# Linear attention with a block-diagonal state: both heads' sequential and low-rank products padded with zeros to the whole 128x128 array

## The chip, the cores and the metric

The kernel runs on one core of a Trainium2 chip. The metric is the device time of one execution in microseconds. TensorE is PE in the rows (PEld its weight loads), VectorE is DVE, ScalarE is ACT, GpSimd is POOL, SyncE is SP and issues the DMAs.

## The reference

256 tokens of width 1024 go through two layers of a block A and then two of a block B. The part that the change touches is one of three branches of the mixing stage of block A, a linear attention with a state (RWKV-7): 8 heads of 64 features, and per head a 64x64 state that is carried over the tokens.

```python
def wkv7_scan(r, decay, k, v, a, b):
...
    def step(state, inp):
        r_t, w_t, k_t, v_t, a_t, b_t = inp
        sa = jnp.einsum('bhij,bhj->bhi', state, a_t)
        state = (state * w_t[:, :, None, :] + sa[..., None] * b_t[:, :, None, :]
                 + v_t[..., None] * k_t[:, :, None, :])
        return state, jnp.einsum('bhij,bhj->bhi', state, r_t)
...
    w = -jax.nn.softplus(-(w0 + jnp.tanh(xw) @ w_up)) - 0.5
    a = jax.nn.sigmoid(a0 + xa @ a_up)
```

The last two lines are the low-rank products: `xw` and `xa` have 64 features each.

## The kernel before

Features lie on partitions, tokens along the free dimension. Every large product is split into three matmuls of reduced-precision halves (lines 164, 165 and 166, `float32r`, 128x128 weights by 256 tokens); this stream of large products runs through the whole kernel. `wload` brings weights by DMA into a ring of buffers, ACT rounds them to `hi` (line 137) and DVE takes the rest `lo` (line 138).

The mixing stage `mix_a` puts small chains of dependent steps between the large products. Each chain is a generator, and `Order` decides in program order where its next step is emitted; the tile scheduler then fixes each engine's order. Four chains `rwkv_pair` per layer do the linear attention, each for two heads on the two halves of the 128 partitions; their products are in `float32`, which the trace records as two passes each. A chain forms the low-rank products (lines 460 and 473, 64 rows by 256 columns), the stacked keys `BK` and queries `AR`, the products inside the four chunks of 64 tokens (line 539), a triangular inverse `Q` by doubling (lines 582 and 590, products of 64x64), and then walks the chunks in order. In the walk each chunk reads the state `ST` (line 609, one product per head, each followed by its own addition into `W`, line 611), multiplies by the inverse (line 616, copied to `U` by line 618), updates the state (line 624; lines 628 to 631 on DVE) and forms the output (lines 636 and 638, in turn for each head, copied to `y` by line 640).

A head occupies 64 partitions, so these products use a quarter or a half of the array; `tile_size` of an instruction (64x64, 128x64, 64x128 or 128x128, rows by columns) says which form the array then has. The form stands in the rows as 64\*64 and so on. PSUM banks of the chains are `rec`, two in turn. The state is kept as [(head, feature), 64], the two heads under each other.

## Time and profile before

| what | value |
| --- | --- |
| median of 3 runs | 2324.88 us (2322.84 to 2325.23) |
| span of the profiled execution, first to last instruction | 2323.2 us |
| PE busy | 2240.6 us, 96% of the span |
| DVE busy | 1677.5 us, 72% |
| ACT busy | 1276.9 us, 55% |
| the chain that ended last | 80% PE, 8% DMA, 7% DVE, 4% ACT |

The profiled execution's span is its own time without what lies around the first and last instruction; the median of the runs is 1.7 us above it. Matmuls overlap in the pipeline, so durations of PE rows overlap too: what a product costs the stream is read from the starts of the rows, not from their durations. A start in the timeline is in microseconds from the span's start, and a row with xN merges N records.

### The profile page before, as it was taken

The numbers are of one execution on the slowest core, as the hardware profiler recorded it, in microseconds if no ns is written. First come the engines' busy times: TensorE is split into PE (matmuls) and PEld (weight loads), VectorE is DVE, ScalarE is ACT, GpSimd is POOL, SyncE is SP. The second block draws the span as 40 slices with busy tenths as digits, with TensorE's granted clock in tenths as the row PEclk, the third lists the DMA queues.
The fourth block names the chain that finished last, engine by engine and source line by source line (L and its number), as shares of the span: only waits on it lengthen the run. The fifth ranks groups of instructions, "written<-read, shape, count | busy, mean of one in ns | idle before, by whom it ended". The sixth has DMA issues, their size and how long they took to land.

```text
span 2323.2 us, 46766 instructions
## 1 busy us (share of the span) xinstructions
PE 2240.6 (96%) x19122; PEld 2142.4 (92%) x19122; DVE 1677.5 (72%) x3026; ACT 1276.9 (55%) x2144; POOL 0.2 (0%) x4
## 2 busy tenths in 40 slices
PE   4999998978999999999999999999999999999999
PEld 4888898978888889999999999899999999999999
DVE  7777767757677776877576659976667655997665
ACT  4574545544457464565454457654455446666444
POOL 0000000000000000000000000000000000000000
PEclk9999999989999999999999999999999999999999
DMA  7634457777663445875576563466565556346653
GB/s 294 190 118 128 142 177 242 250 199 231 191 199 116 137 129 167 266 228 159 169 237 182 161 208 109 131 211 186 156 210 183 174 168 200 109 138 216 183 158 124
DMA packets 129117, 416.69 MB, mean 179 GB/s; under 512 B 14564, under 2 KB 20324, under 8 KB 128134
## 3 DMA queue, kind: packets, MB, share of 16 engines
q1 hardware_dynamic: 126718, 409.50, 55.8%
q10 hardware_dynamic: 2184, 4.19, 0.9%
q8 instruction: 150, 2.46, 0.4%
q14 instruction: 65, 0.53, 0.1%
HBM read 408.40 MB, written 5.24 MB: 178 GB/s over the span
## 4 chain that ended last, share of the span: by engine, by line
PE 80%; DMA 8%; DVE 7%; ACT 4%; issue 1%; SPq 0%; ACTq 0%; DVEq 0%
PE ps L164 23%; PE ps L165 22%; PE ps L166 22%; DMA raw<-in_ffn_up 3%; DVE lo L138 2%; DMA raw<-in_w_ada 2%; ACT hi L137 1%; DMA raw<-in_w_in 1%; PE rec L582 1%; PE rec L590 1%; DVE raw L369 1%; PE rec L1178 1%; DVE raw L338 1%; PE rec L636 1%; PE ps L191 1%
## 5 line engine op out<-in xcount | busy, mean ns | idle before, releaser
L164 PE MATMUL ps<-h,hi 128*128 128x256 f32 x5080 | 1438.4, 284 | 31.9 <-ACT h L201 29.6
L166 PE MATMUL ps<-h,lo 128*128 128x256 f32 x5080 | 1433.4, 283 | 14.7 <-DVE lo L138 14.7
L165 PE MATMUL ps<-l,hi 128*128 128x256 f32 x5080 | 1435.7, 283 | 4.9 <-DVE l L202 4.7
L137 ACT CAST hi<-raw 128x1024 fp32r<-128x1024 f32 (+1 forms) x724 | 704.7, 977 | 648.4 <-PE ps L165 377.8
L138 DVE TENSOR_TENSOR lo<-raw,hi 128x1024 fp32r<-128x1024 f32 (+1 forms) x724 | 818.9, 1133 | 301.6 <-ACT hi L137 299.0
L164 PEld LDWEIGHTS ps<-h,hi 128*128 128x128 f32 x5080 | 961.0, 190 | 47.2 <-ACT h L201 31.9
L166 PEld LDWEIGHTS ps<-h,lo 128*128 128x128 f32 x5080 | 962.3, 190 | 23.8 <-DVE lo L138 15.7
L165 PEld LDWEIGHTS ps<-l,hi 128*128 128x128 f32 x5080 | 961.8, 189 | 13.9 <-DVE l L202 6.8
L201 ACT CAST h<-t 128x256 fp32r<-128x256 f32 x172 | 68.6, 403 | 122.8 <-DVE t L996 96.1
L338 DVE SCALAR_TENSOR_TENSOR raw<-raw,cact 128x1024 f32<-128x1024 f32 x80 | 97.2, 1215 | 35.4 <-DMA raw<-in_w_ada 35.4
L202 DVE TENSOR_TENSOR l<-t,h 128x256 fp32r<-128x256 f32 x172 | 72.3, 423 | 60.5 <-ACT h L201 59.9
L993 DVE TENSOR_TENSOR t<-ps,r 128x512 f32<-128x512 f32 x88 | 60.8, 690 | 41.7 <-PE ps L166 41.3
L1183 DVE SCALAR_TENSOR_TENSOR cy<-cp,cwh,cy 128x256 f32<-128x256 f32 x192 | 85.0, 476 | 3.2 <-ACT cy L1181 2.9
L215 ACT ACTIVATE t<-x 128x256 f32<-128x256 f32 x96 | 38.5, 407 | 15.4 <-DVE x L964 8.5
L222 DVE TENSOR_TENSOR t<-t,t 128x256 f32<-128x256 f32 x87 | 36.4, 418 | 5.5 <-ACT t L215 4.3
L191 PE MATMUL ps<-hi,l 128*128 128x256 f32 x128 | 37.7, 294 | 0.0
L190 PE MATMUL ps<-hi,h 128*128 128x256 f32 x128 | 37.7, 294 | 0.0
L996 DVE TENSOR_TENSOR t<-t,t 128x256 f32<-128x256 f32 x88 | 36.8, 418 | 1.0 <-ACT t L995 1.0
L995 ACT ACTIVATE t<-t 128x256 f32<-128x256 f32 x88 | 36.2, 411 | 0.9
L192 PE MATMUL ps<-lo,h 128*128 128x256 f32 x128 | 36.7, 287 | 0.0
L960 ACT ACTIVATE t<-t 128x256 f32<-128x256 f32 x44 | 18.1, 415 | 29.0 <-DVE t L959 29.0
L416 ACT ACTIVATE t<-t,sh,am 128x256 f32<-128x256 f32 x32 | 18.1, 595 | 26.0 <-DVE am L395 22.5
(311 smaller groups left out, 1884.3 us busy)
## 6 DMA issues: line engine op xcount, KB each, us to landing
raw<-in_w_in SPq DMA_DIRECT2D x176, 512.0 KB, 4.2
raw<-in_ffn_in SPq DMA_DIRECT2D x176, 512.0 KB, 4.2
raw<-in_ffn_up SPq DMA_DIRECT2D x88, 512.0 KB, 5.4
raw<-in_w_ada SPq DMA_DIRECT2D x84, 512.0 KB, 4.8
raw<-in_ffn_out SPq DMA_DIRECT2D x64, 384.0 KB, 3.1
raw<-in_ffn_out SPq DMA_DIRECT2D x64, 320.0 KB, 3.2
raw<-in_w_branch SPq DMA_DIRECT2D x24, 512.0 KB, 4.1
raw<-in_ffn_down SPq DMA_DIRECT2D x32, 384.0 KB, 3.2
```

Of the source, the lines that this page charges most:

```text
L137: nc.scalar.copy(hi[:, :m], raw[:, :m])
L138: nc.vector.tensor_tensor(lo[:, :m], raw[:, :m], hi[:, :m], SUB)
L164: mm(ps, w[0], x[0], start=first, stop=False)
L165: mm(ps, w[0], x[1], start=False, stop=False)
L166: mm(ps, w[1], x[0], start=False, stop=last)
L191: mm(ps[:, :256], x[k][1][:, sl], h, start=False, stop=False)
L201: nc.scalar.copy(h, src)
L202: nc.vector.tensor_tensor(l, src, h, SUB)
L215: nc.scalar.square(sq, x[k])
L338: nc.vector.scalar_tensor_tensor(raw, raw, 1.0, cact, MUL, MUL, accum_out=mods[f // 8][:, f % 8:f % 8 + 1])
L993: nc.vector.tensor_tensor(v3(gu, 2), v3(ps, 2), rb, MUL)
L1183: stt(y, cp[:, jj:jj + S], cwh[:, jj * 4 + i:jj * 4 + i + 1], y, MUL, ADD)
```

## The change

The state of a pair becomes [128, 128] with the two heads on its diagonal blocks and zeros elsewhere, kept so by a multiplication with the block mask `blk` (whose 1/64 is undone by a factor 64 in `Pe`). One product for both heads then takes the place of two: the read of the state is one 128x128 product with both `a` and `r` as columns (half of its result is not used) and one addition for both heads; the inverse is applied to both heads at once, with a persistent, zeroed `wz` in place of `W`; state update and output are one product each, of which the diagonal blocks are copied out by two half-size copies. `AR`'s chunk order and the group order of `AT` are turned so that the operands lie together. The low-rank weights are padded with zeros to 128 rows (`lora`, zeroed on GpSimd ahead of two DMAs of 64 rows), and both products go into one bank. The bonus block `rkb` is made in the chain, and some buffer counts fall.

```diff
@@ -349,12 +349,14 @@
-        self.lora = p.tile([128, 512], F32, tag="lora", name=G.nm("lora"), bufs=1)
+        self.lora = p.tile([128, 2, 512], F32, tag="lora", name=G.nm("lora"), bufs=1)
+        nc.gpsimd.memset(self.lora, 0.0)
@@ -371,7 +373,8 @@
-        G.nc.sync.dma_start(self.lora, G.ins["lora"][self.l])
+        for i in range(2):
+            G.nc.sync.dma_start(self.lora[64 * i:64 * i + 64, i, :], G.ins["lora"][self.l][64 * i:64 * i + 64, :])
@@ -433,11 +436,11 @@
-BUFS = dict(P=1, iP=1, kkn=1, kp=1, BK=1, AR=2, bv=2, uv=8, SA=1, SR=2, BT=2, AT=2, Q=4, R=2, X=2, Y=2, W=2, ST=3, y=2)
-def rwkv_pair(G, L, mp, p, zk, zr, zv, zwa, tw, sg, out, O):
+BUFS = dict(P=1, iP=1, kkn=1, kp=1, BK=1, AR=2, bv=2, uv=8, SA=1, SR=2, BT=2, AT=2, Q=4, R=1, X=1, Y=1, ST=2, y=2)
+def rwkv_pair(G, L, mp, p, zk, zr, zv, zwa, sg, out, O):
@@ -454,12 +457,18 @@
+    def ch2(t):
+        return t.rearrange("p (c t j) -> p c t j", t=2, j=64)
...
-    mm(ps[:, :S], L.lora[0:64, p * 128:p * 128 + 128], tw[0:64, :], start=True, stop=True)
+    for i in range(2):
+        mm(ps[:, i * S:(i + 1) * S], L.lora[:, i, p * 128:p * 128 + 128], zwa, start=True, stop=True)
     yield 0.6
...
+    ag = G.tmp(S)
+    act(ag, ps[:, S:], AF.Tanh, scale=0.5, bias=L.a0h[:, p:p + 1])
@@ -467,11 +476,7 @@
-    ag = G.tmp(S)
-    ps = G.rec()
-    mm(ps[:, :S], L.lora[64:128, p * 128:p * 128 + 128], zwa[64:128, :], start=True, stop=True)
-    act(ag, ps[:, :S], AF.Tanh, scale=0.5, bias=L.a0h[:, p:p + 1])
@@ -497,28 +502,32 @@
     yield 0.8
...
-    stt(AR[:, :, 0, 1:], ch(kkn)[:, :, 1:], -1.0, ch(P)[:, :, :63], MUL, MUL)
-    ts(AR[:, :, 0, 0:1], ch(kkn)[:, :, 0:1], -1.0, None, MUL)
-    tt(AR[:, :, 1, :], ch(zr), ch(P), MUL)
+    AR4 = AR.rearrange("p (c t) s j -> p c (t s) j", t=2)
+    for t in range(2):
+        stt(AR4[:, :, 1 + t, 1:], ch2(kkn)[:, :, t, 1:], -1.0, ch2(P)[:, :, t, :63], MUL, MUL)
+    ts(AR4[:, :, 1:3, 0:1], ch2(kkn)[:, :, :, 0:1], -1.0, None, MUL)
+    tt(AR4[:, :, 0::3, :], ch2(zr), ch2(P), MUL)
...
-    nc.vector.tensor_copy(Pe, ch(P)[:, :, 63])
+    nc.vector.tensor_scalar(Pe, ch(P)[:, :, 63], 64.0, None, MUL)
     yield 1.0
...
-    mm(ps[:, :S], L.rkblk[p], rk, start=True, stop=True)
+    rkb = mp.tile([128, 128], F32, tag="rkb", name=G.nm("rkb"), bufs=2)
+    ts(rkb, G.c("blk", 128), 64.0, L.col("r_k", p), MUL, MUL)
+    mm(ps[:, :S], rkb, rk, start=True, stop=True)
     yield 0.6
...
     yield 0.3
@@ -540,15 +549,16 @@
-            p4 = pss[h].rearrange("p (c s j) -> p c s j", s=2, j=64)
-            tt(o[:, h, :, :], p4[:, :, i, :], G.c("smask", 128)[:, 64 * i:64 * i + 64].unsqueeze(1).to_broadcast([128, 4, 64]), MUL)
+            p4 = pss[h].rearrange("p (c s j) -> p c s j", s=4, j=64)
+            tt(o[:, h, :, :].rearrange("p (c t) j -> p c t j", t=2), p4[:, :, 1:3, :] if i == 0 else p4[:, :, 0::3, :],
+               G.c("smask", 128)[:, 64 * i:64 * i + 64].unsqueeze(1).unsqueeze(1).to_broadcast([128, 2, 2, 64]), MUL)
...
-    WV = big("W", [2, 128])
+    WV = L.wz[p % 2]
@@ -556,10 +566,11 @@
-    nc.scalar.copy(WV.rearrange("p c j -> p (c j)"), ps[:, :S])
+    nc.scalar.copy(WV[64:128, 0::2, :], v3(ps[64:128, :S], 2))
+    nc.scalar.copy(WV[0:64, 1::2, :], v3(ps[0:64, :S], 2))
...
-    at = AT.rearrange("p (h t) j -> p h t j", t=2)
+    at = AT.rearrange("p (t h) j -> p h t j", t=2)
@@ -595,52 +606,48 @@
     yield 0.5
...
     for c in range(4):
         bu = 64 if c % 2 == 0 else 0
         U = UV[c]
-        Wc = WV[bu:bu + 64, c // 2, :]
+        Wc = WV[bu:bu + 64, c, :]
         if ST is not None:
-            for h in range(2):
-                bs = 64 * h
-                psw = G.rec()
-                mm(psw[bu:bu + 64, 0:64], AR[bs:bs + 64, c, 0, :], ST[bs:bs + 64, :], start=True, stop=True)
-                yield 0.4
-                tt(Wc[:, bs:bs + 64], psw[bu:bu + 64, 0:64], Wc[:, bs:bs + 64], ADD)
+            psw = G.rec()
+            mm(psw[:, 0:128], AR[:, c, :, :].rearrange("p s j -> p (s j)"), ST, start=True, stop=True)
+            yield 0.4
+            tt(Wc, psw[bu:bu + 64, 0:128], Wc, ADD)
         yield 0.4
         psu = G.rec()
+        mm(psu[:, 0:128], Q[:, c // 2 * 2:c // 2 * 2 + 2, :].rearrange("p a b -> p (a b)"), WV[:, c, :], start=True, stop=True)
+        yield 0.5
...
-            mm(psu[bu:bu + 64, bs:bs + 64], Q[bu:bu + 64, 2 * h + c // 2, :], Wc[:, bs:bs + 64], start=True, stop=True)
-        yield 0.5
-        nc.vector.tensor_copy(U[bu:bu + 64, :], psu[bu:bu + 64, :128])
+            nc.vector.tensor_copy(U[bu:bu + 64, bs:bs + 64], psu[bs:bs + 64, bs:bs + 64])
         yield 0.4
         if c < 3:
...
-            for h in range(2):
-                bs = 64 * h
-                mm(pss[bs:bs + 64, 0:64], BT[:, c, bs:bs + 64], U[:, bs:bs + 64], start=True, stop=True)
+            mm(pss[:, 0:128], BT[:, c, :], U, start=True, stop=True)
             yield 0.5
-            nST = big("ST", [64])
+            nST = big("ST", [128])
             if ST is None:
-                ts(nST, pss[:, :64], Pe[:, c:c + 1], None, MUL)
+                stt(nST, pss[:, 0:128], Pe[:, c:c + 1], G.c("blk", 128), MUL, MUL)
             else:
-                tt(nST, pss[:, :64], ST, ADD)
-                ts(nST, nST, Pe[:, c:c + 1], None, MUL)
+                tt(nST, pss[:, 0:128], ST, ADD)
+                stt(nST, nST, Pe[:, c:c + 1], G.c("blk", 128), MUL, MUL)
         psy = G.rec()
+        mm(psy[:, 0:128], U, SR[:, :, c, :], start=True, stop=ST is None)
+        if ST is not None:
+            mm(psy[:, 0:128], ST, AR[:, c, c % 2:c % 2 + 1, :].to_broadcast([128, 2, 64]), start=False, stop=True)
+        yield 0.4
...
-            o = psy[bs:bs + 64, 0:64]
-            mm(o, U[:, bs:bs + 64], SR[:, h, c, :], start=True, stop=ST is None)
-            if ST is not None:
-                mm(o, ST[bs:bs + 64, :], AR[bs:bs + 64, c, 1, :], start=False, stop=True)
-        yield 0.4
-        nc.scalar.copy(y[:, c * 64:c * 64 + 64], psy[:, :64])
+            nc.scalar.copy(y[bs:bs + 64, c * 64:c * 64 + 64], psy[bs:bs + 64, bs:bs + 64])
         if c < 3:
             ST = nST
...
     yield 0.8
@@ -745,23 +752,20 @@
-    L.rkblk = []
-    for p in range(4):
-        t = mp.tile([128, 128], F32, tag=f"rkb{p}", name=G.nm("rkb"))
-        nc.vector.tensor_scalar(t, G.c("blk", 128), 64.0, L.col("r_k", p), MUL, MUL)
-        L.rkblk.append(t)
...
         return G.fpair(G.wload(w_in[l, i], 2048), h, 8, (0, 1024))
...
+    L.wz = [mp.tile([128, 4, 128], F32, tag=f"wz{i}", name=G.nm("wz")) for i in range(2)]
+    for t in L.wz:
+        nc.gpsimd.memset(t, 0.0)
...
     first = G.fmulti(pre or [G.wload(w_in[l, i], 2048) for i in (12, 6)], h, 8, (0, 1024))
...
-    tw = zwa
-    act(tw[0:64, :], zwa[0:64, :], AF.Tanh)
+    act(zwa[0:64, :], zwa[0:64, :], AF.Tanh)
```

The walk of the second pair in layer 0, on PE, at the first read of the state. Names are tile_number<-inputs; `ps` rows are the large products. It stood so before:

```order
L636 MATMUL rec_2422<-SR_1432,uv_1403 64x64 x2
L165 MATMUL ps_2467<-l_1314,hi_2457 128x256
L609 MATMUL rec_2426<-ST_2420,AR_1296 64x64
L166 MATMUL ps_2467<-h_1313,lo_2458 128x256
L164 MATMUL ps_2467<-h_1636,hi_2457 128x256
L165 MATMUL ps_2467<-l_1637,hi_2457 128x256
L166 MATMUL ps_2467<-h_1636,lo_2458 128x256
L164 MATMUL ps_2467<-h_1794,hi_2457 128x256
L165 MATMUL ps_2467<-l_1795,hi_2457 128x256
L609 MATMUL rec_2432<-ST_2420,AR_1296 64x64
L616 MATMUL rec_2439<-W_1465,Q_2342 64x64
L166 MATMUL ps_2467<-h_1794,lo_2458 128x256
```

The same place on PE stands so now:

```order
L166 MATMUL ps_2451<-h_1312,lo_2442 128x256
L641 MATMUL rec_2410<-SR_1433,uv_1405 128x128
L619 MATMUL rec_2414<-ST_2408,AR_1295 128x128
L164 MATMUL ps_2451<-h_1631,hi_2441 128x256
L165 MATMUL ps_2451<-l_1632,hi_2441 128x256
L166 MATMUL ps_2451<-h_1631,lo_2442 128x256
L164 MATMUL ps_2451<-h_1784,hi_2441 128x256
L165 MATMUL ps_2451<-l_1785,hi_2441 128x256
L166 MATMUL ps_2451<-h_1784,lo_2442 128x256
L164 MATMUL ps_2451<-h_1925,hi_2441 128x256
L624 MATMUL rec_2420<-wz_325,Q_2331 128x128
L593 MATMUL rec_2428<-R_2422,X_2424 64x64 x8
```

The read of the state (L609, now L619) was two products of 64x64 at two places and is one of 128x128; the product with the inverse (L616, now L624) is one too and stands seven large products behind it.

The output of the next chunk on PE, a little further on. It stood so before:

```order
L164 MATMUL ps_2467<-h_1938,hi_2457 128x256
L165 MATMUL ps_2467<-l_1939,hi_2457 128x256
L166 MATMUL ps_2467<-h_1938,lo_2458 128x256
L636 MATMUL rec_2499<-SR_1432,uv_1404 64x64
L638 MATMUL rec_2499<-AR_1296,ST_2420 64x64
L636 MATMUL rec_2499<-SR_1432,uv_1404 64x64
L638 MATMUL rec_2499<-AR_1296,ST_2420 64x64
L609 MATMUL rec_2505<-ST_2496,AR_1296 64x64
L164 MATMUL ps_2533<-h_1313,hi_2463 128x256
L165 MATMUL ps_2533<-l_1314,hi_2463 128x256
```

The same place on PE stands so now:

```order
L166 MATMUL ps_2451<-h_1784,lo_2442 128x256
L164 MATMUL ps_2451<-h_1925,hi_2441 128x256
L165 MATMUL ps_2451<-l_1926,hi_2441 128x256
L166 MATMUL ps_2451<-h_1925,lo_2442 128x256
L641 MATMUL rec_2481<-SR_1433,uv_1406 128x128
L643 MATMUL rec_2481<-AR_1295,ST_2408 128x128
L619 MATMUL rec_2488<-ST_2478,AR_1295 128x128
L164 MATMUL ps_2512<-h_1312,hi_2447 128x256
L165 MATMUL ps_2512<-l_1313,hi_2447 128x256
```

The output was four products that took turns between two forms of the array (L636, L638), with a read of the state behind them; it is two whole-array products (L641, L643), with the read right behind.

Counted over the whole order of PE, the array goes between the whole form and a part of it 498 times before and 296 times now, and from one part form straight into another 107 times before and 6 times now. Of the two heads' reads of the state (L609), 9 of the 24 pairs stand side by side before; of the state updates (L624), 22 of the 24 do.

## Rows read from the trace of the kernel before

**Rows 1.** The page: busy time, share of the span, instructions.
```profile
PE 2240.6 (96%) x19122; PEld 2142.4 (92%) x19122; DVE 1677.5 (72%) x3026; ACT 1276.9 (55%) x2144; POOL 0.2 (0%) x4
```

**Rows 2.** Busy time by stretch, then granted clock, DMA share, GB/s: PE, PEld, DVE, ACT, POOL.
```profile
84.00:340.00 256.00, 254.93 (x2489) 222.81 (x2489) 186.51 (x425) 141.66 (x260) 0.00 (x0) 1.00 0.45 142
340.00:640.00 300.00, 267.92 (x2138) 263.24 (x2137) 209.81 (x362) 148.31 (x242) 0.00 (x0) 0.93 0.71 224
664.00:930.00 266.00, 264.94 (x2588) 232.28 (x2589) 194.55 (x441) 147.30 (x267) 0.00 (x0) 1.00 0.45 143
```

**Rows 3.** Who PE waited for, 84 to 340 us, longest first: total, times, longest.
```profile
PE rec L262 <- ACT t L478: 0.3, 1, 0.3
```

**Rows 4.** PE in order of time around one L609: start, duration, line, form.
```profile
132.66 0.28 PE L164 MATMUL ps<-h,hi 128*128 128x256 f32 x1
132.87 0.33 PE L609 MATMUL rec<-ST,AR 64*64 64x64 f32 x2
...
133.35 0.28 PE L166 MATMUL ps<-h,lo 128*128 128x256 f32 x1
```

**Rows 5.** PE in order of time around one L616, the two heads together.
```profile
325.12 0.28 PE L164 MATMUL ps<-h,hi 128*128 128x256 f32 x1
325.33 0.44 PE L616 MATMUL rec<-W,Q 64*64 64x64 f32 x4
...
325.93 0.28 PE L166 MATMUL ps<-h,lo 128*128 128x256 f32 x1
```

**Rows 6.** PE in order of time around one output group, L636 and L638.
```profile
327.70 0.28 PE L166 MATMUL ps<-h,lo 128*128 128x256 f32 x1
327.90 0.33 PE L636 MATMUL rec<-SR,uv 128*64 128x64 f32 x2
...
329.16 0.28 PE L165 MATMUL ps<-l,hi 128*128 128x256 f32 x1
```

**Rows 7.** PE around a whole-array float32 pair, L248, 128 columns each; first, a run of large ones.
```profile
393.04 0.28 PE L165 MATMUL ps<-pj,hi 128*128 128x256 f32 x1
...
393.63 0.28 PE L164 MATMUL ps<-pj,hi 128*128 128x256 f32 x1
393.75 0.60 PE L248 MATMUL aux<-ca,rc 128*128 128x128 f32 x4
...
394.31 0.28 PE L166 MATMUL ps<-pj,lo 128*128 128x256 f32 x1
```

**Rows 8.** PE around one whole-array float32 product, L645, 256 columns.
```profile
330.33 0.28 PE L166 MATMUL ps<-h,lo 128*128 128x256 f32 x1
330.45 0.59 PE L645 MATMUL rec<-y,ca 128*128 128x256 f32 x2
...
331.00 0.28 PE L165 MATMUL ps<-l,hi 128*128 128x256 f32 x1
```

**Rows 9.** PE around one low-rank product, L460.
```profile
182.03 0.28 PE L164 MATMUL ps<-h,hi 128*128 128x256 f32 x1
182.24 0.70 PE L460 MATMUL rec<-z,lora 64*128 64x256 f32 x2
...
183.09 0.28 PE L166 MATMUL ps<-h,lo 128*128 128x256 f32 x1
```

**Rows 10.** DVE and ACT by line and shape: evacuations, and the nearest form.
```profile
L611 DVE TENSOR_TENSOR W<-rec,W 64x64 f32<-64x64 f32 x48 | 9.7, 216 | 15.3 <-PE rec L609 15.0
...
L821 DVE SCALAR_TENSOR_TENSOR bsp<-aux,lnb,bsp 128x128 f32<-128x128 f32 x8 | 2.8, 349 | 2.4 <-PE aux L819 2.4
...
L640 ACT COPY y<-rec 128x64 f32<-128x64 f32 x32 | 6.7, 210 | 20.2 <-PE rec L638 16.7 <-PE rec L636 1.8 <-PE rec L609 1.4
```

**Rows 11.** All engines in order of time: one read of the state.
```profile
312.13 0.35 DVE L611 TENSOR_TENSOR W<-rec,W 64x64 f32<-64x64 f32 x2 [0.38 <-PE rec L609]
...
312.40 1.21 DVE L138 TENSOR_TENSOR lo<-raw,hi 128x1024 fp32r<-128x1024 f32 x1
...
312.81 0.33 PE L616 MATMUL rec<-W,Q 64*64 64x64 f32 x2
```

More of the change, by code (lines that the diff above doesn't have):

```diff
@@ L783, in start @@
     def start(p):
-        O.add(f"r{p}", rwkv_pair(G, L, mp, p, zkr[p][:, 0, :], zkr[p][:, 1, :], zv[p], zwa, tw, sg, yr, O), 1.0)
+        O.add(f"r{p}", rwkv_pair(G, L, mp, p, zkr[p][:, 0, :], zkr[p][:, 1, :], zv[p], zwa, sg, yr, O), 1.0)
     def values(i):
```

## Prediction

> **What bounds the kernel now.** I read the page first: PE is busy 96% of the span [rows 1]. Such a busy share hides what PE is busy with, so the second view is the busy time by stretch. The linear attention lies in two stretches of about 260 us, one per layer; there PE is busy 254.93 of 256 us and 264.94 of 266 us at the full clock, DVE 73% and ACT 55% [rows 2]. The third view, the waits, says that in the first of them PE's longest wait was 0.3 us [rows 3]. So in these stretches the end is set by how long PE takes over its own list, and a product that costs the stream less ends the stage earlier by as much. Between them (340 to 640 us) it is otherwise: PE idles 32 of 300 us and the DMA share is 0.71 [rows 2].
>
> What a small product costs the stream is read from starts. Large products start 0.118 us apart: 393.04 and 393.63 are six starts, five spacings [rows 7]. The reader takes the start of the last large product ahead of a small group and of the second one behind it, and subtracts two spacings (0.236).
> - One L609 alone: 133.35 - 132.66 - 0.236 = 0.454 us [rows 4].
> - Two L616 in the same part of the array: 325.93 - 325.12 - 0.236 = 0.574 us [rows 5], 0.12 more than one. So a 64-column product itself takes about 0.116 us, and the other 0.338 us of a lone one is paid at its edges, 0.169 at each change between the whole array and a part of it (the gap ahead alone is 0.21 us, where 0.118 is usual).
> - The output group, which takes turns between 128\*64 and 64\*64: 329.16 - 327.70 - 0.236 = 1.224 us [rows 6]. Less four products (0.464) and the two edges (0.338), three inner changes are left at 0.141 each.
> - Two whole-array float32 products of 128 columns: 394.31 - 393.63 - 0.236 = 0.444, 0.222 each [rows 7], with 0.118 us ahead as between large products and no edge. One of 256 columns: 331.00 - 330.33 - 0.236 = 0.434 [rows 8].
> - One low-rank product (64 rows by 256 columns): 183.09 - 182.03 - 0.236 = 0.824, or 0.486 without its edges [rows 9].
>
> **The change part by part, on PE.** Counts come from four pairs in each of two layers, four chunks (three that read a state, three that update it) and two heads: so 4 x 2 x 4 x 2 = 64 L636, and 48 L609. Those of the changes of form come from the order.
> 1. Edges removed: 498 - 296 = 202 of 0.169 us: 34.1 us. Inner changes removed: 107 - 6 = 101 of 0.141: 14.2 us.
> 2. Products removed, their own time: 48 L609, of which 9 pairs run side by side, so 39 x 0.116 = 4.5; 64 L616, 7.4; 48 L624, 22 pairs side by side, 26 x 0.116 = 3.0; 64 L636 and 48 L638 in turn, 13.0; 16 low-rank ones at 0.486, 7.8. Together 35.7 us.
> 3. Products added: 24 reads, 32 inverse products, 24 updates and 56 output products, 136 whole-array ones of 128 columns, 136 x 0.222 = 30.2 us; 16 low-rank ones of 256 columns, 16 x 0.434 = 6.9. Together 37.1 us.
>
> Net: 34.1 + 14.2 + 35.7 - 37.1 = 46.9 us less on PE. The padding by itself buys nothing (35.7 against 37.1); all of the gain is changes of form.
>
> The padded product is not in the trace with a block-diagonal operand or a broadcast one. Its bounds are the 0.116 us of a 64-column product from below, which would add 136 x 0.106 = 14.4 us to the gain, and the 0.434 us of a 256-column one from above, which would take 28.8 us from it. I take 0.222, since that row has exactly 128 rows, 128 columns and a float32 operand.
>
> One read per head costs 0.454 us alone, two 64-column products of one part 0.116 us each and 0.338 at their edges, and one whole-array product for both heads 0.222 without an edge [rows 4, 5, 7]; by the rows, then, filling the array is the cheaper form here. The Trainium skill speaks against the change: "TensorEngine Tiling (Array Packing)", section When to Use Tiling, sends products with a contraction or a free size of 64 to parts of the array, for up to twice the throughput. By that rule without edges the sum of the three points would be 37.1 - 35.7, or 1.4 us slower; by the rows it is 46.9 us faster. The same page's section Key Properties says that changing the tiling mode drains TensorE, which the edges in the rows bear out.
>
> **The change on the other engines.** On DVE, 48 additions of 64x64 at 0.216 us become 24 of 64x128, and 32 copies of 64x128 become 64 of 64x64 [rows 10]. Shapes that are missing I bound by that 0.216 from below and by the 0.349 of a 128x128 three-operand form from above, and take 0.28 (the middle) for 64x128, 0.22 for 64x64 and 0.349 for the masked state update: -3.6, +5.1 and some +3 us over both layers, with the split of `AR`, eight more instructions of 0.22 at least, some 6 us. ACT has 32 more small copies and 8 split ones: at 0.21 each about +7. Neither decides: DVE's 187 us in a stretch become 190 in some 234, from 73% to 81%, hidden behind PE. If that cover were gone, the cost would be those 6 and 7 us.
>
> The zeroing on POOL (two `lora`, four `wz`) and the second DMA of `lora` add no bytes; POOL is otherwise idle (0.2 us in all [rows 1]). The zeroing stands ahead of uses that come tens of microseconds later, so I cost it at nothing; without cover, six of them at the largest elementwise time in the rows (1.21 us, DVE, [rows 11]) would be 7 us. Buffers of `R`, `X`, `Y` fall to one and of `ST` to two; each is read by a product that PE finishes before the step that overwrites it can have its input, so nothing waits that did not.
>
> **What is late next.** The chain has become short in PE time, but its DVE steps have not. In the rows, DVE stood idle for 0.38 us until a read had ended, its two additions took 0.35 us, a `lo` of 1.21 us came next in its queue, and the L616 that needs the additions started 0.68 us after they had begun [rows 11]. Now five to seven large products (0.6 to 0.8 us) and the 0.222 us of the read lie between read and inverse at the tight places; the addition of some 0.28 us fits in, but not where a `lo` is ahead of it. A wait here blocks the large products behind it on PE. There are 112 such links (24 read to inverse, 32 inverse to the next, 24 update to read, 32 output to copy); I put 3 us on them, between nothing and the rival below. Another 1.5 us is lost where PE has idle time anyway: the low-rank products of each layer's first pair stand ahead of the two stretches.
>
> Sum: 46.9 - 3 - 1.5 = 42.4 us. The profiled span 2323.2 becomes 2280.8; the median of the runs is 1.7 us above the span, so **2282.5 us**.
>
> **The rivals.**
> - *The chain's waits come forward.* If the 112 links wait 0.2 us each on average, 22 us go back: 2305 us. For it: DVE at 81% with pieces of 1.21 us. Against: the distances in the order are much as before, and PE waited almost never [rows 3].
> - *The DMA-bound stretch behind layer 0 swallows its half.* If the 300 us between the stages kept their end because transfers set it, 21 us would be lost: 2304 us. For it: 32 us of PE idle there [rows 2]. Against: those transfers are issued as ring buffers come free in program order, so they move forward with the stage.
> - *No change.* If the 0.338 us were paid by any small product that breaks into the stream, whatever its form, or if the new products brought edges of their own, only the products' own time would change: 37.1 added against 35.7 removed, 2326 us. Against: 0.12 us ahead of the whole-array ones [rows 7, 8] and 0.20 or 0.21 ahead of the others [rows 4 to 6, 9]. This is also what the Trainium skill's section on when to tile, named above, would lead to; the rows do not bear it out.
> - *Slower.* One mechanism: DVE's queue. The links wait for evacuations that stand behind `lo` pieces. It decides from 46.9 / 112 = 0.42 us a link; at 0.5 us, 56 us come back: 2334 us. Against: the mean would have to be a third of a whole `lo`.
> - *More than forecast.* The padded products at the lower bound: 14 us more, 2268 us.
>
> **How the numbers follow.** Forecast (gain 30 to 50 us) 0.65; waits 0.15; swallowed 0.08; more 0.05; no change 0.04; slower 0.03. The forecast stands alone with 2274 to 2294. To hold 8 in 10 the range reaches down to the lower bound of the padded product, 2268, and up to the two half-gain cases, 2304. Faster by over 0.2% (4.6 us, about what a measurement of this kernel can tell from no change): 0.65 + 0.15 + 0.08 + 0.05 = 0.93; within it 0.04; slower 0.03.
>
> **What would show it.** Right: around the new read (L619) the large products keep 0.118 us ahead and the group costs about 0.22 us; the output pair (L641, L643) costs 0.44 where it was 1.22; each stretch of linear attention is some 20 us shorter with PE busy throughout and DVE near 80%. Wrong: a lone padded product that costs 0.4 us or has a gap of 0.2 us ahead of it (price or edges), new PE waits for DVE in the walk (chain), or shorter stages with a longer stretch between them (DMA).

## The result and the profile after

The changed kernel takes 2294.28 us (median of 4 runs, 2293.05 to 2297.13) where the one before took 2325.06 beside it (4 runs, 2322.84 to 2326.48): ratio 0.9868, 95% interval 0.9856 to 0.9881, 31 us faster. The forecast was 2282.5: the gain was to be 42.4 us. The profiled execution's span fell from 2323.2 to 2295.3 us, by 27.9 and not by 31, because the execution that was profiled after the change is the slowest of its four (2297.13). The page and the same stretches as in [rows 1, 2]:

```profile
span 2295.3 us, 46372 instructions
PE 2206.4 (96%) x18850; PEld 2131.8 (93%) x18850; DVE 1685.2 (73%) x3042; ACT 1286.4 (56%) x2184; POOL 4.2 (0%) x10
...
84.00:340.00 256.00, 251.16 (x2466) 230.30 (x2465) 200.28 (x452) 154.67 (x290) 0.96 (x1) 1.00 0.50 156
340.00:640.00 300.00, 265.70 (x2124) 260.66 (x2122) 208.12 (x356) 147.75 (x241) 0.99 (x2) 0.94 0.71 222
664.00:930.00 266.00, 262.39 (x2544) 242.06 (x2543) 210.43 (x465) 159.94 (x299) 0.00 (x0) 1.00 0.51 159
```

Two things are to be seen. PE busy fell by 34.2 us, more than the span. And PE, which idled 1.07 of 256 us in the first stretch, idles 4.84 there now, and 3.61 of 266 instead of 1.06 in the second; DVE is at 78% and 79%, near the 81% forecast. The mixing stages end earlier now, so these two windows reach past them; cut at the stages' ends (84 to 321 and 657 to 896 us) PE still idles 3.66 of 237 and 2.98 of 239 us.

Where nothing holds them up, the padded products cost what the prediction took. PE in order of time around an output pair and around a read that nothing holds up:

```profile
270.24 0.28 PE L166 MATMUL ps<-h,lo 128*128 128x256 f32 x1
270.36 0.38 PE L641 MATMUL rec<-SR,uv 128*128 128x128 f32 x2
270.57 0.39 PE L643 MATMUL rec<-AR,ST 128*128 128x128 f32 x2
...
270.92 0.28 PE L165 MATMUL ps<-l,hi 128*128 128x256 f32 x1
...
711.33 0.28 PE L164 MATMUL ps<-h,hi 128*128 128x256 f32 x1
711.45 0.38 PE L619 MATMUL rec<-ST,AR 128*128 128x128 f32 x2
...
711.79 0.28 PE L166 MATMUL ps<-h,lo 128*128 128x256 f32 x1
```

The pair costs 270.92 - 270.24 - 0.236 = 0.444 us, where [rows 6] had 1.224; the read 711.79 - 711.33 - 0.236 = 0.224, with 0.12 us ahead of it, where [rows 4] had 0.454 and 0.21. But of the 16 reads that stand alone between large products only three cost less than 0.27, and six cost 0.458 to 0.604. A lone padded product at 0.4 us was one of the signs by which the forecast was to be wrong in the price; experiment 4 tells price and wait apart.

The gain of a stage is not swallowed behind it. DVE's additions that end the mixing stage (L922, now L926), in before and then after, first and last start:

```profile
L922 DVE SCALAR_TENSOR_TENSOR x<-ps,gt,x x16: 474/477/485, 367.1 to 971.7; 128x256 f32<-128x256 f32 x16
```
```profile
L926 DVE SCALAR_TENSOR_TENSOR x<-ps,gt,x x16: 477/479/485, 350.8 to 943.5; 128x256 f32<-128x256 f32 x16
```

Layer 0 is 16.3 us ahead when these begin; the last addition of its feed-forward starts at 601.30 instead of 616.57, still 15.3 ahead; layer 1 brings it to 28.2, and 27.9 are left at the end of the span.

**Where the rest is.** From the starts of all matmul records I took, for each kernel, what the groups of small products cost in the mixing stage of both layers ("small groups"), as the prediction did, and beside it their list price. A stage is taken from shortly before the first doubling product to shortly after the last gate product (7.0 us more, over both layers, than between these two). The list price is: the products' own times from undisturbed groups (0.222 for 128 columns of the whole array, 0.434 for 256, 0.116 for one of 64 columns, and so on), 0.169 for each edge and 0.141 for each inner change. What the list does not explain is the rest. A late group is one that costs over 0.06 us more than its list price; the last column has what is late in groups that begin 0.046 to 0.060 or 0.140 to 0.150 us after a DVE or ACT instruction ends, the two distances that most of the late ones have. All in us, one profiled execution each; how far a rest varies from execution to execution is not known.

| kernel | both stages | small groups | list | rest | late right behind DVE or ACT |
| --- | --- | --- | --- | --- | --- |
| before | 510.2 | 230.8 | 228.0 | 2.9 | 4.0 |
| after | 479.5 | 199.0 | 180.5 | 18.5 | 15.8 |
| before, output by form | 499.2 | 219.6 | 221.2 | -1.6 | 4.2 |
| before, without links | 509.9 | 229.4 | 227.7 | 1.7 | 3.5 |
| before, three banks | 502.8 | 222.4 | 220.2 | 2.2 | 7.0 |
| after, output in parts | 490.2 | 209.6 | 200.1 | 9.5 | 8.6 |
| after, without links | 483.1 | 201.9 | 181.2 | 20.7 | 17.0 |
| after, three banks | 479.1 | 201.6 | 179.1 | 22.5 | 22.0 |
| after, shared banks | 482.8 | 202.3 | 182.5 | 19.9 | 18.7 |
| after, no links, three banks | 474.0 | 195.8 | 180.2 | 15.7 | 15.9 |
| after, walk apart (161 more large products in the stages) | 499.3 | 196.7 | 180.9 | 15.8 | 14.7 |
| after, all chains apart (213 more) | 524.6 | 220.7 | 177.9 | 42.8 | 43.9 |
| after, copies split | 484.9 | 202.8 | 180.8 | 22.1 | 20.8 |
| after, rounding on POOL | 501.9 | 222.6 | 183.7 | 38.9 | 34.2 |

The list shrank by 47.5 us, against 46.9 forecast. The list uses the prediction's own prices, so this agreement is one of counts; that the prices hold after the change too is seen from the groups that are not late, which together cost 2.3 us less than their list (20.8 us of late groups, a rest of 18.5). 15.6 us came back as a rest that the kernel before did not have. Of these, 11.8 are late starts right behind DVE or ACT (15.8, where the kernel before has 4.0); the other 3.8 hang on the prices of the list. The two distances are no accident: in after, about four in five of the late groups begin at one of them, and about one in five of the others. The 15.8 us are 9.7 behind DVE and 6.1 behind ACT. What these groups wait for was the question of the experiments.

### The profile page after: what moved, and what is told of

Read it like the earlier page. It is cut to its first block, busy times and chain, and to the rows that moved or that the text cites. A ratio compares the mean times of both kernels' runs of the same rounds, so it can differ in the third digit from the quotient of the medians.

```text
span 2295.3 us, 46372 instructions
## 1 busy us (share of the span) xinstructions
PE 2206.4 (96%) x18850; PEld 2131.8 (93%) x18850; DVE 1685.2 (73%) x3042; ACT 1286.4 (56%) x2184; POOL 4.2 (0%) x10
## 4 chain that ended last, share of the span: by engine, by line
PE 77%; DMA 9%; DVE 7%; ACT 5%; issue 1%; SPq 0%; ACTq 0%; DVEq 0%
PE ps L164 22%; PE ps L165 22%; PE ps L166 22%; DVE lo L138 3%; DMA skew<-ohb 2%; ACT hi L137 2%; DMA raw<-in_ffn_up 2%; DMA raw<-in_w_ada 2%; DMA raw<-in_w_in 1%; PE rec L601 1%; PE rec L593 1%; DVE raw L371 1%; DMA raw<-in_w_out 1%; PE rec L1182 1%; PE aux L1044 0%
## 5 line engine op out<-in xcount | busy, mean ns | idle before, releaser
L164 PE MATMUL ps<-h,hi 128*128 128x256 f32 x5080 | 1437.1, 284 | 31.0 <-ACT h L201 28.5
L166 PE MATMUL ps<-h,lo 128*128 128x256 f32 x5080 | 1433.2, 283 | 15.4 <-DVE lo L138 15.4
L164 PEld LDWEIGHTS ps<-h,hi 128*128 128x128 f32 x5080 | 959.7, 189 | 44.1 <-ACT h L201 30.8
L419 ACT ACTIVATE t<-t,sh,am 128x256 f32<-128x256 f32 x32 | 18.1, 596 | 26.5 <-DVE am L398 22.5
```

The source lines that it names most:

```text
L164: mm(ps, w[0], x[0], start=first, stop=False)
L166: mm(ps, w[1], x[0], start=False, stop=last)
```

## The experiments

**1. The form alone, in the kernel before.** The four output products of a chunk, which took turns between 128x64 and 64x64, are issued with like forms together:

```diff
         for h in range(2):
...
-            mm(o, U[:, bs:bs + 64], SR[:, h, c, :], start=True, stop=ST is None)
-            if ST is not None:
-                mm(o, ST[bs:bs + 64, :], AR[bs:bs + 64, c, 1, :], start=False, stop=True)
+            mm(psy[bs:bs + 64, 0:64], U[:, bs:bs + 64], SR[:, h, c, :], start=True, stop=ST is None)
+        if ST is not None:
+            for h in range(2):
...
+                mm(psy[bs:bs + 64, 0:64], ST[bs:bs + 64, :], AR[bs:bs + 64, c, 1, :], start=False, stop=True)
```

> The kernel before with one edit: the four output products of a chunk are issued by form (both heads' L636, then both heads' L638) instead of in turn; the products, their number and all evacuations stay. In the order the inner changes of form fall from 107 to 59, the edges stay 498. Theory of the forms (a change of form costs by itself, 0.141 us inside a group): 48 x 0.141 = 6.8 us faster, about 2318 us. Rival (the gain of the change comes from fewer products, fewer steps and fewer evacuations): no change, 2325 us.

Measured: 2312.34 us (6 runs), ratio 0.9949 (0.9932 to 0.9966), 12 us faster. PE around one such group:

```profile
281.26 0.28 PE L166 MATMUL ps<-h,lo 128*128 128x256 f32 x1
281.47 0.34 PE L635 MATMUL rec<-SR,uv 128*64 128x64 f32 x4
281.73 0.33 PE L639 MATMUL rec<-AR,ST 64*64 64x64 f32 x4
...
282.22 0.28 PE L165 MATMUL ps<-l,hi 128*128 128x256 f32 x1
```

It costs 282.22 - 281.26 - 0.236 = 0.724 us, not 1.224 [rows 6], with the same four products. The two changes less are 0.28 of the 0.50. Without its two edges and one inner change the group keeps 0.245 us, 0.061 for each of the four products, where two in the same part of the array take 0.116 each [rows 5]: like products of the two heads, on two parts of the array, run side by side (their records start 0.006 us apart), which the expectation had left out. The rival, no change, falls: with the same products, steps and evacuations, order alone gave 12 us, somewhat over half of it by fewer changes of form and the rest by products side by side. (The list of the table fell by 6.8 us only, for the changes of form; that it holds nothing for products side by side fits its rest of -1.6.)

**2 and 3. The links of the walk.** In both kernels the products of the walk read slices of `BT` in place of what the step before has just evacuated (after: lines 615, 619, 643; the evacuations write to rows that nothing reads):

```diff
-        U = UV[c]
+        U = BT[:, 3 - c, :]
...
-            mm(psw[:, 0:128], AR[:, c, :, :].rearrange("p s j -> p (s j)"), ST, start=True, stop=True)
+            mm(psw[:, 0:128], AR[:, c, :, :].rearrange("p s j -> p (s j)"), BT[:, 3 - c, :], start=True, stop=True)
...
```

> The changed kernel with the chain of the walk cut: read, update and output products take operands that are ready long before (slices of BT), and the additions and copies of the walk write to rows that nobody reads; so the walk computes something else. Products, forms and evacuations keep their number and size. Theory of the waits (some 16 us of the 47 us that PE's list lost came back as waits for DVE and ACT, about 11 of them in the walk): 8 to 12 us faster than the changed kernel, about 2284 us. Rival (the padded products or the edges that are left cost more than priced): within 3 us of the changed kernel's 2294 us.

> The kernel before with the chain of the walk cut in the same way: products take ready operands, additions and copies write to rows that nobody reads; the walk computes something else. Theory of the waits (before, the edges of the small products left DVE and ACT the time they needed): within 3 us of 2325 us. Rival (the walk waited as much before as after): 8 us or more faster.

Measured: after 2293.8 us, ratio 0.987 (0.9851 to 0.9889); before 2322.92, ratio 0.9993 (0.9979 to 1.0006). Neither moved; the first one's rest is 20.7, where after has 18.5. That the operand links of the walk alone are the cause is refuted. The time is the one that the rival named (price or edges dearer than taken); experiment 4 speaks against that rival. Who the read waited for, in after and then without the links:

```profile
L619 PE MATMUL rec<-ST,AR x48: 270/275/377, 130.9 to 882.1; 128*128 128x128 f32 x48
...
its engine sat idle before it (us, times) until:
  issue: 0.9, 4
  ACT Y L596: 0.7, 2
  ACT y L647: 0.5, 2
```
```profile
L619 PE MATMUL rec<-BT,AR x48: 275/275/580, 131.7 to 880.4; 128*128 128x128 f32 x48
...
its engine sat idle before it (us, times) until:
  ACT y L647: 1.0, 4
```

`Y` and `y` are copies out of `rec` banks, and the read has neither as an operand. In after the view names these copies or nobody ("issue"), and never the state, although experiment 4 shows a read that starts right behind the state's evacuation; with the operand gone, the read still waits behind a copy out of a bank.

**4. The output in parts again.** Everything of the change stays but the output, which is formed per head on parts as before (296 edges become 346, 6 inner changes 81):

```diff
-        mm(psy[:, 0:128], U, SR[:, :, c, :], start=True, stop=ST is None)
...
-            mm(psy[:, 0:128], ST, AR[:, c, c % 2:c % 2 + 1, :].to_broadcast([128, 2, 64]), start=False, stop=True)
...
+            mm(o, U[:, bs:bs + 64], SR[:, h, c, :], start=True, stop=ST is None)
...
+                mm(o, ST[bs:bs + 64, bs:bs + 64], AR[bs:bs + 64, c, c % 2, :], start=False, stop=True)
...
```

> The changed kernel with one part undone: the output products are again one per head on parts of the array, in turn, with one copy to y; state, read, inverse and update stay whole. In the order the edges go from 296 to 346 and the inner changes from 6 to 81. Theory of the forms: 50 x 0.169 + 75 x 0.141 + 13.0 - 12.4 = 19.6 us more of PE's list, of which the waits that it covers give some back: 12 to 20 us slower than the changed kernel, 2306 to 2314 us. Rival (number of steps and evacuations decides): 56 more products but 32 fewer copies, within 4 us of 2294 us.

Measured: 2300.9 us, ratio 0.9895 (0.9877 to 0.9914): 6.6 more than after, outside both numbers (the two ratios' intervals just overlap). The table tells why: the list grew by the 19.6 us expected, the stages by 10.7 only, and the rest fell from 18.5 to 9.5. All 17 reads that stand alone now cost 0.219 to 0.253 us. The read is the same padded product as in after, so what made it dear there is not its price: that rival, of experiment 2 too, falls. One link from update to read, the last pair of layer 0 at its third chunk, all engines, in after:

```profile
305.08 0.23 DVE L628 COPY uv<-rec 64x64 f32<-64x64 f32 x1
305.34 1.23 DVE L138 TENSOR_TENSOR lo<-raw,hi 128x1024 fp32r<-128x1024 f32 x1
...
305.45 0.46 PE L632 MATMUL rec<-uv,BT 128*128 128x128 f32 x2
...
306.60 0.29 DVE L638 TENSOR_TENSOR ST<-rec,ST 128x128 f32<-128x128 f32 x1
306.92 0.35 DVE L639 SCALAR_TENSOR_TENSOR ST<-ST,Pe,ca 128x128 f32<-128x128 f32 x1
307.14 0.28 PE L166 MATMUL ps<-h,lo 128*128 128x256 f32 x1
...
307.42 0.46 PE L619 MATMUL rec<-ST,AR 128*128 128x128 f32 x2
...
307.84 0.28 PE L165 MATMUL ps<-l,hi 128*128 128x256 f32 x1
```

and the same link with the output in parts:

```profile
310.98 1.23 DVE L138 TENSOR_TENSOR lo<-raw,hi 128x1024 fp32r<-128x1024 f32 x1
...
311.09 0.46 PE L632 MATMUL rec<-uv,BT 128*128 128x128 f32 x2
...
312.23 0.29 DVE L638 TENSOR_TENSOR ST<-rec,ST 128x128 f32<-128x128 f32 x1
...
312.56 0.35 DVE L639 SCALAR_TENSOR_TENSOR ST<-ST,Pe,ca 128x128 f32<-128x128 f32 x1
...
313.67 0.28 PE L166 MATMUL ps<-h,lo 128*128 128x256 f32 x1
...
313.91 0.38 PE L619 MATMUL rec<-ST,AR 128*128 128x128 f32 x2
```

In both a `lo` of 1.23 us stands ahead of the state's two evacuations, and the state is ready 1.82 us after the update began. In after the read's turn comes before that, and it starts 0.15 us behind the evacuation's end, at a cost of 307.84 - 307.14 - 0.236 = 0.464. With the output in parts the read's turn comes 2.82 us after the update, and it finds the state ready for a microsecond. So the expensive output products had been covering DVE: of 19.6 us of list that this version adds, 9 stand in time that PE would have waited. The wait is shown for this link, and the cheaper reads bear it out; that the rest's other half comes about in the same way is inferred from the late starts.

**5 to 7. The banks.** Three `rec` banks and three for the large products instead of two and four, in both kernels; and, in after, two products that follow each other in the halves of one bank:

```diff
-PBANKS = (4, 2, 2)
+PBANKS = (3, 2, 3)
```
```diff
...
-        psu = G.rec()
+        psu = G.rec() if ST is None else psw
...
-        psy = G.rec()
+        psy = (pss if c < 3 else G.rec())[:, 128:256]
```

> The changed kernel with three PSUM banks for the small chains (rec) and three for the large products, instead of two and four. Cutting the walk's operands loose gained nothing, so the time that was expected and did not come is not in the links. Theory of the banks (a small product waits until DVE or ACT has emptied the bank that it takes over, which the edges covered before): some 16 us of such waits mostly go, and the order has 12 edges less (2 us): 10 to 16 us faster than the changed kernel, 2278 to 2284 us. Rival (the edges and padded products that are left cost more than priced): only the order's 2 us, about 2292 us. Three banks for the large products may cost something in either.

> The kernel before with three banks for rec and three for the large products. Its order has 440 edges instead of 498 and 115 inner changes instead of 107: 58 x 0.169 - 8 x 0.141 = 8.7 us less. Theory of the banks (before, hardly a wait for banks): that and no more, about 2316 us. Rival (banks cost as much before as after): another 10 us or more, 2306 us or less.

> The changed kernel, with two of the walk's products in one bank: read and inverse in two halves of one, update and output in two halves of another, so that the walk takes over half as many banks; the output products then also wait for DVE's first reading of the update. Theory of the banks: 4 to 10 us faster than the changed kernel, 2284 to 2290 us, less what the new wait costs. Rival (price of edges and products): the order has 8 edges and 4 inner changes more, 2 us slower, about 2296 us.

Measured: after with three banks 2305.79 us, ratio 0.9914 (0.9889 to 0.9938); before with three banks 2325.45, ratio 1.0 (0.9985 to 1.0016); shared banks 2297.94, ratio 0.9874 (0.9849 to 0.9898). The rest stayed at 22.5 and 19.9, so banks alone are refuted too. The 8 us by which the first one's span is longer lie outside the stages, whose length is that of after; there the large products have a bank less, and in the stretch behind layer 0 they wait for DVE's evacuations of the feed-forward (a row that after does not have among its longest):

```profile
PE ps L164 <- DVE t L965: 21.4, 6, 12.4
```

The kernel before with three banks missed its theory (2316 us) as well as its rival, and yet its stages confirm the price of the edges: the order has 58 edges less and 8 inner changes more, the list fell by 7.8 us, and the small groups by 8.4 (230.8 to 222.4), which made the stages 7.4 us shorter. The time outside them grew by as much, with the same wait (L961 there is L965 of the changed kernel):

```profile
PE ps L164 <- DVE t L961: 22.4, 6, 11.8
```

**8. Links and banks together.** The edits of 2 and 5 in one kernel.

> Both at once: the products of the walk read values that are there long before (what they compute is then no linear attention), and the small groups have three banks and the large products three. 292 edges and 8 inner changes. If the same late evacuation is waited for twice, as an operand and as the bank that it frees, then neither edit alone helps but both together do: the unexplained 18 to 22 us of the two stages fall below 12, and the stages are 8 us shorter than the 479 of the kernel with three banks alone (the time outside grows by 11 as there): about 2297. Rival (neither is the cause): unexplained 18 or more, 2304 to 2306.

Measured: 2302.0 us, ratio 0.9901 (0.988 to 0.9921); stages 474.0, 5 shorter than with three banks alone; rest 15.7. That is between the theory (under 12) and its rival (18 or more), and settles neither; 3 us less than after is not clear of what such kernels differ by, since with the walk apart (below), where links and banks stay, the rest is 15.8 too. The groups outside the walk keep their waits (8.4 of the 15.7 us), and inside it a product can still wait behind a copy out of a bank. The inverse products of this kernel:

```profile
L624 PE MATMUL rec<-wz,Q x64: 270/275/377, 116.3 to 880.6; 128*128 128x128 f32 x64
...
its engine sat idle before it (us, times) until:
  ACT y L647: 2.0, 6
```

**9 and 10. The distance.** The walk's steps further apart in program order, and then all chains. (Of the first, the steps of 0.4 became 0.655 in the kernel that ran, not the 0.55 that its expectation names; those of 0.5 became 0.65.)

```diff
-            yield 0.4
+            yield 0.655
```
```diff
-PACE = (0.8, 1.5)
+PACE = (1.0, 1.5)
```

> The distances between the steps of the walk are lengthened by 0.15 each (0.4 to 0.55, 0.5 to 0.65), nothing else; 288 edges and 18 inner changes (296 and 6), which by themselves would make 0.3 us. Theory: the 18 us that the list of PE does not explain in the stages are waits for evacuations, each of which costs the stream what is missing between its latency and the large products that stand between; the groups of the walk hold 8 of them, and about half go: 2290 (2287 to 2292), with fewer reads and inverse products above 0.3 us. Rival (the delay does not depend on the distance): 2294, within 2.

> All chains of the stage are set 25% further apart (pace 0.8 to 1.0); 274 edges and 16 inner changes, by themselves 2.3 us less. Theory of the waits for evacuations: 6 to 10 of the 18 us go as well, 2282 to 2286. Rival (distance does not matter): 2292. A third way: the last chain then ends behind the large products, and the stage's end is bare; then 2294 to 2300 with PE idle near the end of each stage.

Measured: the walk apart 2290.3 us, ratio 0.9858 (0.9839 to 0.9877), 4 us less than after by its median, but its interval overlaps after's. The walk's groups hold 9.1 us of rest, where they held 8.7: the expected mechanism did not show, and whether this version is faster stays open. All chains apart: 2316.41 us, ratio 0.9953 (0.9935 to 0.997), slower than after by 22. The third way of its expectation happened, and harder. The last 11 us of its two stages:

```profile
341.00:352.00 11.00, 6.26 (x18) 4.20 (x18) 3.72 (x15) 2.32 (x5) 0.00 (x0) 0.51 0.15 48
...
914.00:925.00 11.00, 6.42 (x34) 4.62 (x32) 4.90 (x16) 2.73 (x7) 0.00 (x0) 0.84 0.15 48
```

The chain runs on alone here, 18 and 34 matmuls in 11 us; the granted clock is 0.51 in the first, about the lower of the two levels (1.2 of 2.4 GHz), where PE is busy 6.26 of the 11 us. Distance is limited: what is put between the steps is missing behind the last of them.

**11 and 12. The queues.** One of the two copies of the inverse product goes from DVE to ACT; and the rounding of the weights goes from ACT to POOL.

```diff
-            nc.vector.tensor_copy(U[bu:bu + 64, bs:bs + 64], psu[bs:bs + 64, bs:bs + 64])
+            (nc.scalar.copy if h else nc.vector.tensor_copy)(U[bu:bu + 64, bs:bs + 64], psu[bs:bs + 64, bs:bs + 64])
```
```diff
-            nc.scalar.copy(hi[:, :m], raw[:, :m])
+            nc.gpsimd.tensor_copy(hi[:, :m], raw[:, :m])
```

> Of the two copies of the inverse product's result, which DVE does one behind the other (0.22 us each), one goes to ACT; 294 edges and 10 inner changes, by themselves 0.2 us more. Theory of the waits for evacuations: the 32 updates and outputs get their operand some 0.2 us earlier; where they are late now (8 groups by 0.1 to 0.3 us) 1 to 2 us go: 2292 to 2293. Rival (ACT's queue, with pieces of 1.05 us, is later than DVE's second copy): 2294 to 2298.

> The rounded copies of the weights (hi, 1.05 us each on ACT, whose queue they share with the evacuations) go to POOL, which is idle; the products, their order and the 296 edges stay. Theory: part of the late small groups wait for an evacuation that stands behind such a piece in ACT's queue (6 us of late starts follow the end of an ACT instruction); 2 to 5 us of these go, 2289 to 2292, with ACT's busy time down by some 270 us. Rival (POOL needs longer than ACT for a piece, and the weights become late): 2300 or more, with large products waiting for lo. A third way (the queue hardly matters, only the evacuation's own length): 2293 to 2295.

Measured: copies split 2298.57 us, ratio 0.9883 (0.987 to 0.9897), 4 us more than after by the median, though the intervals overlap. That goes the rival's way (ACT's queue): what is late behind DVE fell from 9.7 to 6.9, and behind ACT rose from 6.1 to 13.9. Rounding on POOL 2422.93 us, ratio 1.043 (1.0409 to 1.0451). ACT's busy time halved (632.8 us, 654 less and not 270), and what is late behind ACT did not fall (7.9), so what the theory expected did not show; behind DVE it rose from 9.7 to 26.3. The time lies in the rival's range (2300 or more), and POOL does need longer for a piece (1.114 us as a mean of all 724, where ACT needs 0.977), but the large products did not wait longer for `lo`: their wait for it fell from 15.4 to 4.0 us. Only 22 of the 127 us are in the stages (501.9 against 479.5); outside them the longest single wait of PE is 42.4 us, for DVE (`PE ps L164 <- DVE t L965: 42.4, 1, 42.4`). DVE became slower where it reads from SBUF. Groups by line with busy us and mean ns of one (L628 in the first stretch alone), in after:

```profile
L137 ACT CAST hi<-raw 128x1024 fp32r<-128x1024 f32 (+1 forms) x724 | 704.8, 977 | 640.2 <-PE ps L165 360.3
...
L202 DVE TENSOR_TENSOR l<-t,h 128x256 fp32r<-128x256 f32 x172 | 72.5, 424 | 66.1 <-ACT h L201 65.7
...
L628 DVE COPY uv<-rec 64x64 f32<-64x64 f32 x32 | 7.0, 220 | 2.5 <-PE rec L624 2.0
```

and with the rounding on POOL:

```profile
L137 POOL CAST hi<-raw 128x1024 fp32r<-128x1024 f32 (+1 forms) x724 | 804.6, 1114 | 1571.1 <-PE ps L165 1197.8
...
L202 DVE TENSOR_TENSOR l<-t,h 128x256 fp32r<-128x256 f32 x172 | 140.7, 822 | 46.1 <-ACT h L201 45.9
...
L628 DVE COPY uv<-rec 64x64 f32<-64x64 f32 x32 | 7.1, 220 | 2.3 <-PE rec L624 1.8
```

The copy out of PSUM kept its 220 ns, while `l` (two SBUF operands) went from 424 to 822. Not all SBUF work suffered alike: the `lo` pieces of 128x1024, two operands too, went from 1219 to 1232 ns in the first stretch (84 to 340 us), and a copy of 128x256 with one SBUF operand (L492) from 292 to 654 over the whole kernel. The Trainium skill's "GPSIMD Engine Reference", section Specifications, says that GpSimd contends for SBUF with DVE instructions that have two SBUF inputs or run in a 2-port perf mode; the rows of `l` agree, and whether L492 runs in such a mode no run shows. For the question here: with the same products on PE and a slower DVE the rest rises, from 18.5 to 38.9. That fits waits for evacuations, whose own times hardly changed but which stand behind slower work in DVE's queue.

## Why the prediction was right, and by how much it was not

- **Edges, inner changes, own times (46.9 us): right.** The counts are those of the order (the list of the stages shrank by 47.5); the prices are borne out by undisturbed padded products at 0.224 and 0.444, by 12 us from order alone, without any padding (experiment 1), and by the 8.4 us that 58 edges less took from the small groups (experiment 6). "The padding by itself buys nothing" stands; the rival by which any small product pays the edges is refuted.
- **The other engines: right.** The added shapes took 0.282 (64x128), 0.220 (64x64) and 0.343 us (masked state), where 0.28, 0.22 and 0.349 were taken; DVE's busy time grew by 7.7 us in all and ACT's by 9.5, where 6 and 7 were taken. Neither bounds by its busy time; what their queues cost is the term "what is late next" below. POOL's zeroing made its busy time 4.2 us, and the page names no wait for it.
- **The stretch behind layer 0: right.** 15.3 of its 16.3 us arrive at the end of the feed-forward; the rival that swallows them is refuted.
- **"What is late next": mis-sized.** The term was 3 us; the rest rose by 15.6, of which 11.8 are late starts right behind DVE or ACT. With 15.6 in place of 3 the prediction's sum gives 46.9 - 15.6 - 1.5 = 29.8 us, or 2295.1, and 2294.28 was measured; so this term is about the whole miss of 11.8 us. The mechanism is the one named, shown for one link: a wait on PE for an evacuation, where a `lo` is ahead of it (experiment 4). Two steps of the argument failed. "The distances in the order are much as before" is true in program order and false in time: from update to read of the last pair's chunks there were 2.95 and 2.48 us in before and there are 2.24 and 1.97 in after, while DVE's part of it grew, and the output group between them shrank from 1.224 to 0.444. "PE waited almost never" [rows 3] said that there was slack, not how much. And 112 links were too few: of the 18.5 us about half lie in the walk (8.7), the others in the doubling (3.8), the norms and the gate (2.5) and the remaining groups (3.7). By these late starts a shorter list exposes the chains that run beside it, also the ones that the change does not touch.
- **The other 1.5 us** (first pair's low-rank products, where PE idles anyway) no run isolates. The stages became 30.7 us shorter and the profiled span 27.9; where the 2.8 between them were lost is open.
- **The rival of the waits** gave 2305 at 0.2 us a link; it took 22 us off a sum from which 3 were off already, so by its own numbers it is 2302. The rest that came is 15.6 / 112 = 0.14 a link, spread over more than the links, so the result lies between forecast and this rival. It is 0.3 us outside the 2274 to 2294 that the forecast had for itself; the stated range held because it was stretched to 2304 for the two rivals that lose half the gain.
- **Open:** how the rest splits between operands, banks and queues. Without the walk's operand links, or with more banks, it stayed as large; with both it was 3 us smaller and the stages 5.5 shorter, which is not enough to tell. That one late evacuation is waited for in more than one way is a guess that fits, and no run shows it. The queues were never emptied: both edits moved work between them and made the rest larger. `R`, `X`, `Y` and `ST` with the buffers of before were not tried. The traces give no sign that they matter: the idle time of DVE that ends with the product before its write of `X` is 5.6 us with one buffer (L593) and 4.6 with two (L582), and before its write of `R` there is none in either kernel.

The Trainium skill's "TensorEngine Tiling (Array Packing)", section PSUM Bottleneck, says that a faster TensorE leaves the evacuation of PSUM as it was, and that this may then bound. It says so of tiling; here the untiled form was the faster one, and the late starts right behind DVE and ACT, 15.8 us, are in line with the sentence.

## What to carry to other kernels

Where small products stand in a stream of large ones, count the changes of the array's form in the order in which PE gets them, and put like forms together first: that alone gave 12 us in the kernel before, where the whole change gave 31. When the bounding engine's list gets shorter, read each chain beside it anew in time, not in program order: from a product to the next that needs it there must be room for the longest piece in the evacuating queue and the evacuation itself (here 1.82 us from update to state). And an idle engine is only free to take work if it does not slow the busy one.

## What the chip showed that was not expected

- With 0.8 ms of casts on POOL, DVE's two-operand subtraction of 128x256 took 822 ns instead of 424 and its one-operand copy within SBUF 654 instead of 292, the PSUM copy 220 as before.
- Like products of two heads on two parts of the array run side by side: four of 64 columns, in two forms, cost 0.724 us with three changes of form, 0.245 without them.
- Late PE groups start 0.046 to 0.060 or 0.140 to 0.150 us after the end of a DVE or ACT instruction: 15.8 of the 20.8 us of late groups in after are of this kind, and so is the read of experiment 4 (0.15).
- In the kernel before, 58 changes between the whole array and a part of it less (and 8 between two parts more), with the same products, took 8.4 us from the small groups (experiment 6).
